# TensorE instructions in source order inside the long loops of a two-block transformer kernel

## The chip, the cores and the metric

One core of one Trainium2 chip runs the whole program. The metric is device time in microseconds (us), lower is better. TensorE (PE) does every matrix product and every transpose. VectorE (DVE) and ScalarE (ACT) do reductions, exponentials and copies out of PSUM, GpSimd (POOL) a few element-wise steps, and SyncE (SP) issues the transfers.

## The reference

Two transformer blocks on 256 latent tokens (and, in the first layer, 256 context tokens) of width 1024, all in fp32. What matters here, cut down:

```python
def first_block(...):                       # layer 0 and layer 1
    hl, hc = modulate(x_lat, ...), modulate(x_ctx, ...)          # RMS norm with adaptive scale and shift
    mix = even_mixer(...) or odd_mixer(...)                      # layer 0 or layer 1
    x = x + gate * (mix @ w_out[l])
    x = x + gate * conv_ffn(modulate(x), ffn_up, conv, ffn_down) # 1024 -> 2 x 2816 -> 1024
# even_mixer: four recurrent (mLSTM) heads, and eight heads of window attention over 512 tokens
# odd_mixer:  eight heads of global attention, and eight heads of neighbourhood attention with a bias
def window_attention(q, k, v, k_ctx, v_ctx, sink):
    s = [q @ k_ctx, mask(q @ k_band)]
    p = softmax([sink, s])                  # one row per query
    return p @ v
# second_block: mixer A (three dilated groups, merged by their log-sum-exp), layer norm, gate;
#               mixer B (window of 128 with sinks), layer norm, gate
```

## The kernel before, in words

**Products.** Every weight product is made of three matmuls in a reduced fp32 format: a weight is split into a high part (`whi`, cast by ACT at L396) and a low part (`wlo`, subtracted by DVE at L400, by POOL at L398), and hi times hi, hi times lo and lo times hi are summed in PSUM. `gemm_t` (L443, matmuls at L439 to L441 in `mm_t`) holds the weights still and streams the tokens, 512 or 256 columns at a time; `gemm_n` (L477, matmuls at L484 to L486) holds the tokens still. Weights come from memory through SP, 1 MB at a time, into two buffers, and are split in good time. The matmuls of the adaptive norm's parameters (L533, transposes L540) are strewn between.

**Attention.** `_attn_pair` (L841) makes one unit of attention: 128 queries, two heads, 128 to 512 keys. It has three pieces. `probs` issues the scores on PE (L800, L801, a mask at L860), the row maximum on DVE (L867, L870), the exponential on ACT (L882), sums, sinks and the reciprocal on DVE (L872 to L888), and divides the two heads' rows `P` by their sums, on DVE (L900) and on POOL (L901). `turn` transposes `P` on PE (L916, L927) into a tile `t` of PSUM and copies it out as `PT` (L920, L929 on DVE, L931 on ACT). `pv` multiplies `PT` by the values on PE (L937). Mixer A has its own scores (L1633). Tiles of PSUM are few: two for `t`, two for scores `s`, three for products `g`, one for `o`.

**The order of the work.** A hand-made pipe (`_Pipe`, L233) sets the order in which the source issues the pieces. Products call `tick` with their columns, and whenever `pace` columns are through (7000 in window attention, 12000, 9000 and 4000 in layer 1, 10000 in mixer A, 5000 in mixer B), `slot` (L258) issues the next piece of every unit under way, the oldest first, and then the scores of a new one:

```python
    def slot(self):
        for u in list(self.live):
            u.pop(0)()
            if not u:
                self.live.remove(u)
        if self.pending:
            early, u = self.pending.pop(0)
            ...
            u.pop(0)()
            self.live.append(u)
```

So in source order `pv` of one unit, the transposes of the next and the scores of the one after stand together, and between a unit's scores and its transposes there are the products of one or two ticks and the `pv` of the unit before it. In mixer B (`K.lag = 1`) a unit's transposes come one slot later. On top of this a scheduler goes over the whole program: it keeps what depends on what, and orders each engine's list of instructions by its own estimate of when they can start. In the kernel before it does this for all engines everywhere.

Of the kernel before, what the change touches and what calls it, by code (L numbers as in the profile page):

```python
# [10 lines left out]
F32 = mybir.dt.float32  # L11
# [294 lines left out]
class _K:  # L306
    def __init__(self, ctx, tc, aps, out, stop=None, dbg=None):
# [25 lines left out]
        self.sa = rows("sa", 2)  # L333
        self.tm = rows("tm", 6)
        self.n = 0

    def nm(self, s):
        self.n += 1
# [479 lines left out]
def _pow(K, out, ms, n):  # L818
    K.nc.gpsimd.tensor_tensor(out, ms, K.mhalf[:, 0:n], op=ALU.pow)
# [134 lines left out]
def _layer0(K):  # L954
# [3 lines left out]
    with tc.tile_pool(name="h0", bufs=1, reuse_waits="tile") as hp, ExitStack() as es:  # L958
# [32 lines left out]
        with tc.tile_pool(name="att0", bufs=4, reuse_waits="tile") as ap, tc.tile_pool(name="swa", bufs=1, reuse_waits="tile") as sp:  # L991
# [28 lines left out]
                    for t in range(4):  # L1020
                        swa(q, pr, t, o)

            K.pipe.pace = 7000
            _q_gqa(K, sp, H, rows[:, R_SWA:R_SWA + 64], axc, axs, (0, 2), units)
            for T, s in ((kT, 128.0 ** -0.5), (qT, 1.0)):
                for c in range(2):
                    K.gemm_t(K.w(), H, 512, lambda m, g: nc.scalar.activation(T[:, 2 * c + m], g, AF.Copy, scale=s))
            K.pipe.drain()
        with tc.tile_pool(name="mls", bufs=1, reuse_waits="tile") as mp:
            mp = _Rows(mp)  # L1030
            vN = mp.tile([128, 4, 4, 129], F32, name="vN")
# [28 lines left out]
                                                    (slice(4, 8), mixb[x].bitcast(F32))])  # L1060
                return
            st = K.stats(segs)
            _wout(K, 0, mixa, segs, 0, ((256, 512), (0, 256)), st, K.norm(st[0], 0, 1, segs[1], 256))
        K.flush_ada()
        if K.stop == "xm0":
            K.dump("xm0", K.xt)
# [16 lines left out]
def _wout(K, l, mix, segs, k0=0, parts=None, st=None, hooks=()):  # L1083
    nc = K.nc
    t0 = segs[0][0]

    def evac(m, g, lo=0, hi=512):
        for a, b, t in segs:
            if a - t0 < lo or b - t0 > hi:
                continue  # L1090
            x = K.xt[:, m, a:b]
            nc.vector.scalar_tensor_tensor(x, g[:, a - t0:b - t0], K.mod[l][:, 2, t, m:m + 1], x, op0=ALU.mult,
                                           op1=ALU.add)
            if st:
                K.stat_add(st[t], x)

    for c in range(2):
        K.gemm_t(K.w(), mix, segs[-1][1] - t0, lambda m, g, *r: evac(4 * c + m, g, *r), k0, parts if c else None,
                 hooks if c else ())


def _ffn(K, l, segs, st, nxt=None):
# [3 lines left out]
    with tc.tile_pool(name=f"f{l}", bufs=1, reuse_waits="tile") as pool, tc.tile_pool(name=f"fw{l}", bufs=3, reuse_waits="tile") as wx:  # L1106
# [65 lines left out]
                K.gemm_t(K.w(), parts[i], n, lambda m, g, *r: evac(4 * c + m, g, *r), 0, cuts,  # L1172
                         K.norm(st[0], l + 1, 0, segs[1], 256, 3) if st else ())

        K.wide = True
        for i in range(len(FPARTS)):
            up(i)
            if i:
                down(i - 1)
        K.lookahead = 0  # L1180
        K.wide = False
        nst = nxt(segs) if nxt else None
        down(len(FPARTS) - 1, nst)
        K.lookahead = 1
        K.wx = None
        K.flush_ada()
    K.dump(f"x{l}", K.xt)
# [89 lines left out]
def _layer1(K, st):  # L1277
# [5 lines left out]
    with tc.tile_pool(name="l1", bufs=1, reuse_waits="tile") as pool, \  # L1283
# [45 lines left out]
                for t in range(2):  # L1329
                    gqa(q, pr, t, o)  # L1330

        K.pipe.pace = 12000
        _q_gqa(K, pool, H, rows[:, R_GQA:R_GQA + 64], axc, axs, (2,), units)
        kg = pool.tile([128, 64], F32, name="nkg")
        nc.vector.tensor_mul(kg, rows[:, R_NA:R_NA + 64], rows[:, R_NA + 64:R_NA + 128])
        kT = [pool.tile([128, 4, 512], F32R, name=f"nkT{i}") for i in range(2)]
        qT = [pool.tile([128, 8, 256], F32R, name=f"nqT{i}") for i in range(2)]
        def na(pr, t):
            o = _Out(K, 128, 1, 128)
            sl = slice(128 - 128 * t, 256 - 128 * t)  # L1340
            _attn_pair(K, 512, [[x[:, 2 * pr + e, 128 * t:128 * t + 128] for x in qT] for e in range(2)],
                       [[kT[e][:, pr]] * 2 for e in range(2)],
                       lambda e, b: K.xt[:, 2 * b + pr // 2, 128 * (pr % 2) + 64 * e:128 * (pr % 2) + 64 * e + 64],
                       lambda: o()[:, 0], lambda: K.hilo(mix[0][:, 4 + pr, sl], mix[1][:, 4 + pr, sl], o()[:, 0]),
                       bias=lambda e: (256, nb[t][:, 2 * pr + e].rearrange("p k c -> p (k c)")), ident=J)

        for kind, c in ((0, 0), (2, 0), (1, 0), (0, 1), (2, 1), (1, 1)):
            W = K.w()
            for t in ((0, 1) if kind < 2 else (1,)):
                ps = K.pg(128, 2, 256)  # L1350
                for b in range(2):
                    K.gemm_n(W, H, 2 * t + b, ps[:, b])
                if kind == 1:
                    for b in range(2):
                        nc.scalar.copy(K.xt[:, 2 * (2 * t + b) + c, 0:256], ps[:, b])
                    continue
                p8 = ps.rearrange("p b (h d) -> p (b h) d", d=64)
                p4 = ps.rearrange("p b (h d) -> p b h d", d=64)
                ms = _rms8(K, p8, 8, "eighth" if kind == 2 else None)
                rr = K.small([128, 8], "rr")  # L1360
                _pow(K, rr, ms, 8)
                if kind == 0:
                    x = K.e(2, 256)
                    x8 = x.rearrange("p b (h d) -> p (b h) d", d=64)
                    nc.vector.tensor_mul(x8, p8, rr.unsqueeze(2).to_broadcast([128, 8, 64]))
                    nc.vector.tensor_mul(x8, x8, kg.unsqueeze(1).to_broadcast([128, 8, 64]))
                    K.pipe.defer(14000, lambda d=[y[:, 2 * c:2 * c + 2, 256 * t:256 * t + 256] for y in kT], x=x:
                                 _tpose_stack(K, d, x.rearrange("p b (h d) -> p b h d", d=64)))
                    continue
                r4 = rr.rearrange("p (b h) -> p b h", b=2)  # L1370

                def wr(o, hs):
                    for z in range(2):
                        nc.vector.tensor_tensor(o[:, :, :, z], p4[:, :, hs],
                                                r4[:, :, hs].unsqueeze(3).to_broadcast([128, 2, 2, 64]),
                                                op=ALU.mult)

                _stack_k(K, [y[:, 4 * c:4 * c + 4] for y in qT], wr, J)
            if kind == 1:
                for t in range(2):  # L1380
                    for pr in (2 * c, 2 * c + 1):
                        na(pr, t)
                K.pipe.pace = 9000
        K.pipe.settle(8, 8)
        K.pipe.pace = 4000
        _wout(K, 1, mix, lat)
        K.pipe.drain()
        if K.stop == "mix1":
            K.dump("mix1", mix[0].bitcast(F32)), K.dump("mix1l", mix[1].bitcast(F32))
            return  # L1390
# [177 lines left out]
def _block2a(K):  # L1568
# [3 lines left out]
    with tc.tile_pool(name="a2", bufs=1, reuse_waits="tile") as pool, tc.tile_pool(name="aw", bufs=2, reuse_waits="tile") as wx, ExitStack() as es:  # L1572
# [77 lines left out]
        def attn(hg, *a):  # L1650
            for pr in range(2):
                o = _Out(K, 128, 2, 128)
                for t in range(2):
                    unit(hg, pr, t, o, *a)

        K.pipe.pace = 10000
        for hg in range(4):
            attn(hg, *gemms(hg))
        _wout2(K, mx, xp, 0)
        K.pipe.drain()  # L1660
        es.close()
        K.wx = None
        pool2 = _Rows(es.enter_context(tc.tile_pool(name="a2b", bufs=1, reuse_waits="tile")))
# [8 lines left out]
def _block2b(K):  # L1672
# [3 lines left out]
    with tc.tile_pool(name="b2", bufs=1, reuse_waits="tile") as pool, tc.tile_pool(name="b2q", bufs=2, reuse_waits="tile") as qp, \  # L1676
# [63 lines left out]
                       nsink=nsink[:, h2], sink=rows[:, R_BSINK + 2 * kt:R_BSINK + 2 * kt + 2],  # L1740
                       masks=((0, m0),) if t == 0 else ((0, m1),), idm=idb)

        K.pipe.pace = 5000
        K.lag = 1
        for hg in range(4):
            qT = gemms(hg)
            for pr in range(2):
                o = _Out(K, 128, 2, 128)
                for t in range(2):
                    unit(hg, pr, t, o, qT)  # L1750
        _wout2(K, mx, xl, 0)
        K.pipe.drain()
        rb = _wout_ln(K, mx, xl, pool, 1)

        def fin(m, a, b):
# [73 lines left out]
```

## Time and profile before

| | us |
|---|---|
| median of three runs (1650.22 to 1658.45) | 1651.43 |
| the profiled execution | 1659.3 |
| its span | 1657.5 |
| PE busy | 1587.5 (96%) |
| PE loading weights | 1380.9 (83%) |
| DVE busy | 1126.1 (68%) |
| ACT busy | 776.5 (47%) |
| POOL busy | 262.8 (16%) |

Where the stages lie in the span, in us: window attention of layer 0 from 75 to 190, recurrent heads from 217 to 305, FFN from 343 to 740, norm of layer 1 to 760, attention of layer 1 to 925, its FFN to 1132, mixer A from 1180 to 1460, its layer norm and gate to 1535, mixer B to 1610, and the tail. The profile lists, for each engine, when it was busy and what ended each idle time; the table of windows gives busy time in chosen stretches, and a timeline gives single instructions with the idle time before them in brackets. A matmul's row ends later than the next one starts, since matmuls are pipelined: their pace is read from the starts.

### The profile page before, as it was taken

The page shows a single profiled execution, that of the slowest core. Times are in us where ns is not written, and L with a number is a line of the kernel's source. Part 1 is how long each engine was busy: PE and PEld are TensorE (multiplying, and loading weights), DVE is VectorE, ACT ScalarE, POOL GpSimd, SP SyncE. Part 2 cuts the span into 40 slices and gives each one's busy share as a digit, 9 for nine tenths or more (in the row PEclk, how much of TensorE's full clock was granted, in tenths as well). Part 3 has the DMA queues.
Part 4 walks back from the last instruction along what each step waited for, and adds up shares of the span by engine and source line. Part 5 has one row for each costly group of instructions (what it writes and reads, how often), then busy time and mean ns, then how long its engine had stood idle before and what let it go on. Part 6 is the DMA issues. An engine that isn't in the chain of part 4 may idle for free.

```text
span 1657.5 us, 28332 instructions
## 1 busy us (share of the span) xinstructions
PE 1587.5 (96%) x11406; PEld 1380.9 (83%) x11406; DVE 1126.1 (68%) x2169; ACT 776.5 (47%) x1431; POOL 262.8 (16%) x239
## 2 busy tenths in 40 slices
PE   5899999999999999999999899999999999989998
PEld 2777776787777788888888789999999999989887
DVE  4776355576646575577777798777676666677897
ACT  3454344454323333244555555554454554445554
POOL 2321000030000000005231344441010101120111
PEclk9999998999999999998999999999999999989999
DMA  8233321335544432323343355554525352416333
GB/s 333 86 126 103 108 74 59 136 140 175 178 153 176 180 127 102 102 91 94 106 124 128 129 202 187 195 191 157 178 102 179 103 178 102 159 56 214 102 103 102
DMA packets 43475, 229.57 MB, mean 139 GB/s; under 512 B 12552, under 2 KB 15752, under 8 KB 16464
## 3 DMA queue, kind: packets, MB, share of 16 engines
q1 hardware_dynamic: 43344, 227.76, 39.7%
q8 instruction: 90, 1.47, 0.3%
q14 instruction: 41, 0.34, 0.1%
HBM read 226.70 MB, written 1.05 MB: 137 GB/s over the span
## 4 chain that ended last, share of the span: by engine, by line
PE 81%; DVE 9%; DMA 3%; POOL 3%; ACT 3%; issue 2%; SPq 0%; POOLq 0%; DVEq 0%; ACTq 0%
PE g L439 11%; PE g L440 11%; PE g L441 11%; PE g L484 6%; PE g L486 6%; PE g L485 6%; PE s L439 4%; PE s L441 4%; PE s L440 4%; PE o L937 3%; DMA raw<-in_w_dram 3%; PE g L533 3%; DVE wlo L400 2%; PE t L927 2%; PE s L800 1%
## 5 line engine op out<-in xcount | busy, mean ns | idle before, releaser
L396 ACT CAST whi<-raw 128x1024 fp32r<-128x1024 f32 x322 | 332.3, 1048 | 284.2 <-DMA raw<-in_w_dram 179.9
L400 DVE TENSOR_TENSOR wlo<-raw,whi 128x1024 fp32r<-128x1024 f32 x289 | 357.4, 1245 | 141.4 <-ACT whi L396 135.6
L439 PE MATMUL g<-H,whi 128*128 128x256 f32 (+1 forms) x944 | 303.2, 324 | 5.2 <-ACT H L1477 1.8
L440 PE MATMUL g<-H,whi 128*128 128x256 f32 (+1 forms) x944 | 301.8, 320 | 5.5 <-DVE H L630 5.1
L484 PE MATMUL g<-whi,H 128*128 128x256 f32 x1040 | 300.1, 289 | 3.5 <-ACT H L635 2.0
L441 PE MATMUL g<-H,wlo 128*128 128x256 f32 (+1 forms) x944 | 299.3, 318 | 1.7 <-POOL wlo L398 1.7
L486 PE MATMUL g<-whi,H 128*128 128x256 f32 x1040 | 295.7, 285 | 2.4 <-DVE H L639 1.8
L485 PE MATMUL g<-wlo,H 128*128 128x256 f32 x1040 | 294.0, 283 | 0.5 <-DVE wlo L400 0.5
L484 PEld LDWEIGHTS g<-whi,H 128*128 128x128 f32 x1040 | 199.2, 192 | 11.1 <-issue 3.6
L486 PEld LDWEIGHTS g<-whi,H 128*128 128x128 f32 x1040 | 198.6, 191 | 4.8 <-DVE H L639 2.4
L485 PEld LDWEIGHTS g<-wlo,H 128*128 128x128 f32 x1040 | 199.3, 192 | 1.1 <-DVE wlo L400 0.8
L439 PEld LDWEIGHTS g<-H,whi 128*128 128x128 f32 x944 | 177.3, 189 | 26.0 <-issue 4.8
L440 PEld LDWEIGHTS g<-H,whi 128*128 128x128 f32 x944 | 178.3, 189 | 21.7 <-DVE H L630 9.1
L441 PEld LDWEIGHTS g<-H,wlo 128*128 128x128 f32 x944 | 178.0, 189 | 14.8 <-POOL wlo L398 2.1
L901 POOL TENSOR_SCALAR P<-P,rc 128x512 f32<-128x512 f32 (+2 forms) x64 | 55.2, 863 | 500.5 <-DVE rc L1639 263.6
L398 POOL TENSOR_TENSOR wlo<-raw,whi 128x1024 fp32r<-128x1024 f32 x33 | 81.2, 2459 | 100.4 <-ACT whi L396 97.5
L439 PE MATMUL s<-H,whi 128*128 128x256 f32 (+1 forms) x264 | 89.2, 338 | 0.0
L440 PE MATMUL s<-H,whi 128*128 128x256 f32 (+1 forms) x264 | 88.0, 333 | 0.0
L441 PE MATMUL s<-H,wlo 128*128 128x256 f32 (+1 forms) x264 | 87.9, 333 | 0.0
L439 PE MATMUL g<-G,whi 128*128 128x256 f32 (+1 forms) x240 | 78.9, 329 | 3.0 <-DVE e L1124 2.5
L440 PE MATMUL g<-G,whi 128*128 128x256 f32 (+1 forms) x240 | 77.8, 324 | 0.0
L441 PE MATMUL g<-G,wlo 128*128 128x256 f32 (+1 forms) x240 | 77.7, 324 | 0.0
(394 smaller groups left out, 2963.4 us busy)
## 6 DMA issues: line engine op xcount, KB each, us to landing
raw<-in_w_dram SPq DMA_DIRECT2D x209, 1024.0 KB, 4.9
xt<-in_xt_dram SPq DMA_DIRECT2D x1, 2048.0 KB
nab<-in_rpb_dram SPq DMA_DIRECT2D x16, 128.0 KB, 4.0
out_dram<-xt SPq DMA_DIRECT2D x4, 256.0 KB, 2.2
agw<-in_agw_dram SPq DMA_DIRECT2D x1, 512.0 KB, 20.3
mka<-in_tab_dram SPq DMA_DIRECT2D x1, 512.0 KB, 3.5
plr<-in_p_dram SPq DMA_DIRECT2D x2, 256.0 KB, 6.7
e<-in_tab_dram SPq DMA_DIRECT2D x5, 64.0 KB, 4.7
```

Of the source, the lines that this page charges most:

```text
L396: nc.scalar.copy(hi, raw)
L398: nc.gpsimd.tensor_tensor(lo, raw, hi.bitcast(F32), op=ALU.subtract)
L400: nc.vector.tensor_sub(lo, raw, hi.bitcast(F32))
L439: nc.tensor.matmul(out, hi[:, k, s], X[0][:, x], start=f, stop=False)
L440: nc.tensor.matmul(out, hi[:, k, s], X[1][:, x], start=False, stop=False)
L441: nc.tensor.matmul(out, lo[:, k, s], X[0][:, x], start=False, stop=l)
L484: nc.tensor.matmul(out, X[0][:, a + k, s], hi[:, k], start=f, stop=False)
L485: nc.tensor.matmul(out, X[0][:, a + k, s], lo[:, k], start=False, stop=False)
L486: nc.tensor.matmul(out, X[1][:, a + k, s], hi[:, k], start=False, stop=l)
L533: nc.tensor.matmul(acc[g:g + 32], self.sc[:, k, :], raw[:, k], start=(k < 4), stop=(k >= 4))
L901: nc.gpsimd.tensor_scalar(P[1], P[1], rc[:, 1:2], 0.0, op0=ALU.mult, op1=ALU.add)
L937: nc.tensor.matmul(o[64 * e:64 * e + 64], vv(e, b), u["T"][e][:, b], start=(b == 0), stop=(b == kb - 1))
```

## The change

A method `as_written` opens a region in which the scheduler leaves PE's instructions in the order in which the source issues them; the other engines, and the order between engines, stay with it. It is put around the loops of window attention in layer 0 (with the `drain` that empties the pipe), the output product of layer 0, the FFN of both layers, the whole attention of layer 1 with its output product, and the loops of mixers A and B. The norms, the recurrent heads and the layer-norm tails of mixers A and B stay outside. Nothing is added or removed: every engine has the same instructions as before. Names of lines are three to some nine higher in the changed kernel, since lines were added.

```diff
+    def as_written(self):
+        return self.tc.manual_schedule(engines={mybir.EngineType.PE})
...
+            with K.as_written():
+                K.pipe.pace = 7000
+                _q_gqa(K, sp, H, rows[:, R_SWA:R_SWA + 64], axc, axs, (0, 2), units)
...
+                K.pipe.drain()
...
+            with K.as_written():
+                _wout(K, 0, mixa, segs, 0, ((256, 512), (0, 256)), st, K.norm(st[0], 0, 1, segs[1], 256))
...
+        with K.as_written():
+            K.wide = True
+            for i in range(len(FPARTS)):
+                up(i)
+                if i:
+                    down(i - 1)
...
+        with K.as_written():
+            K.pipe.pace = 12000
+            _q_gqa(K, pool, H, rows[:, R_GQA:R_GQA + 64], axc, axs, (2,), units)
...
+            K.pipe.settle(8, 8)
+            K.pipe.pace = 4000
+            _wout(K, 1, mix, lat)
+            K.pipe.drain()
...
+        with K.as_written():
+            K.pipe.pace = 10000
+            for hg in range(4):
+                attn(hg, *gemms(hg))
+            _wout2(K, mx, xp, 0)
+            K.pipe.drain()
...
+        with K.as_written():
+            K.pipe.pace = 5000
+            K.lag = 1
...
+            _wout2(K, mx, xl, 0)
+            K.pipe.drain()
```

**Window attention, PE.** A unit of 512 keys has its scores in tiles `s_321` and `s_322`, its rows in `P_323` and `P_324`, its transposes in `t_327` and `t_329`; `s_333` holds the scores of the next unit, of 256 keys; `g_310` and `g_311` are products. Before:

```order
L801 MATMUL s_322_1681<-kT2_101_534,qT2_122_687 128x512
...
L439 MATMUL g_311_1639<-H0_99,whi_303_1617 128x512
...
L937 MATMUL o_291_1577<-PT_316_1670,v_100_533 64x128
L439 MATMUL g_310_1638<-H0_99,whi_305_1621 128x512
...
L800 MATMUL s_333_1740<-kT2_101_534,qT2_121_686 128x256
...
L440 MATMUL g_310_1638<-H1_100,whi_305_1621 128x512
L927 MATMUL t_327_1724<-ident_83,P_323_1692 128x128 x4
L927 MATMUL t_329_1731<-ident_83,P_324_1693 128x128 x4
L441 MATMUL g_310_1638<-H0_99,wlo_306_1622 128x512
```

Now:

```order
L804 MATMUL s_322_1683<-kT2_101_534,qT2_122_689 128x512
...
L442 MATMUL g_311_1641<-H0_99,whi_303_1619 128x512
...
L940 MATMUL o_291_1579<-PT_316_1672,v_100_533 64x128
L930 MATMUL t_327_1726<-ident_83,P_323_1694 128x128 x4
L930 MATMUL t_329_1733<-ident_83,P_324_1695 128x128 x4
L803 MATMUL s_333_1742<-kT2_101_534,qT2_121_688 128x256
...
L442 MATMUL g_310_1640<-H0_99,whi_305_1623 128x512
```

The transposes have moved ahead of the next unit's scores and of the products `g_310` (eleven of its matmuls stood before them). Between `s_322` and `t_327` there remain the 12 matmuls of `g_311` and the 8 of `pv`.

**The same unit, DVE, in the change.** `wlo_357` and `wlo_359` are low parts of a later weight, `nb` the row maxima.

```order
L873 TENSOR_REDUCE nb_318_1679<-s_321_1682 128x1
L873 TENSOR_REDUCE nb_318_1679<-s_322_1683 128x1
L403 TENSOR_TENSOR wlo_357_1865<-raw_355_1862,whi_356_1864 128x1024
L875 TENSOR_TENSOR nb_318_1679<-nb_318_1679,qnr_120_687 128x2
L403 TENSOR_TENSOR wlo_359_1869<-raw_355_1862,whi_358_1868 128x1024
L877 TENSOR_TENSOR nb_318_1679<-nb_318_1679,nsink_676 128x2
L888 TENSOR_TENSOR es_325_1698<-nb_318_1679,rows_101 128x2
L890 TENSOR_TENSOR ls_319_1680<-ls_319_1680,es_325_1698 128x2
L891 RECIPROCAL rc_320_1681<-ls_319_1680 128x2
L903 TENSOR_SCALAR P_323_1694<-P_323_1694,rc_320_1681 128x512
```

The two subtractions of a weight stand inside the unit's chain, as they did before; what moved is the work of the next unit, whose reduction stood between these rows and now follows them.

**Layer 1, neighbourhood attention, PE.** Here `J` is the matrix that transposes, `s_1502` and `s_1503` are the scores of the next to last unit, `t_1515` and `t_1517` its transposes, `g_1511`, `g_1512` and `g_1525` tiles of the output product (256 columns). Before:

```order
L801 MATMUL s_1503_8437<-nkT1_6973,nqT1_6975 128x512
L439 MATMUL g_1512_8477<-mix10_6770,whi_1468_8290 128x256
...
L927 MATMUL t_1496_8420<-J_6604,P_1491_8387 128x128 x4
L927 MATMUL t_1498_8427<-J_6604,P_1492_8388 128x128 x4
L439 MATMUL g_1525_8536<-mix10_6770,whi_1470_8294 128x256
...
L801 MATMUL s_1522_8520<-nkT1_6973,nqT1_6975 128x512
...
L440 MATMUL g_1525_8536<-mix11_6771,whi_1470_8294 128x256
L927 MATMUL t_1515_8503<-J_6604,P_1504_8446 128x128 x4
L927 MATMUL t_1517_8510<-J_6604,P_1505_8447 128x128 x4
```

Now:

```order
L930 MATMUL t_1496_8431<-J_6613,P_1491_8398 128x128 x4
L930 MATMUL t_1498_8438<-J_6613,P_1492_8399 128x128 x4
L803 MATMUL s_1502_8447<-nkT0_6983,nqT0_6985 128x512
...
L804 MATMUL s_1503_8448<-nkT1_6984,nqT1_6986 128x512
L442 MATMUL g_1511_8474<-mix10_6779,whi_1468_8301 128x256
...
L940 MATMUL o_1513_8502<-PT_1497_8437,xt_87 64x128
L930 MATMUL t_1515_8514<-J_6613,P_1504_8457 128x128 x4
L930 MATMUL t_1517_8521<-J_6613,P_1505_8458 128x128 x4
L803 MATMUL s_1521_8530<-nkT0_6983,nqT0_6985 128x512
```

Each unit's transposes now stand ahead of the next unit's scores, where before they stood behind them. The products between a unit's scores and its transposes are 24 matmuls for this unit, and 12 for the three others of the last four.

**Mixer B, PE.** `s_2714` holds the scores of a unit of 128 keys, `t_2728` its transposes, `t_2719` and `s_2723` belong to the units before and after it, `g_2735` is a product of the next group of heads. Before:

```order
L860 MATMUL s_2714_16116<-mb0b_15623,idb2_15629 128x128
L486 MATMUL g_2735_16202<-whi_2682_15968,H1_100 128x256
...
L860 MATMUL s_2723_16148<-mb1b_15627,idb2_15629 128x256
L484 MATMUL g_2735_16202<-whi_2682_15968,H0_99 128x256
...
L937 MATMUL o_2717_16135<-PT_2709_16108,vb_15693 64x128 x2
L916 MATMUL t_2719_16139<-ident_83,P_2705_16075 128x128 x4
...
L860 MATMUL s_2747_16250<-mb1b_15627,idb2_15629 128x256
L916 MATMUL t_2728_16176<-ident_83,P_2715_16125 128x128 x2
```

Now:

```order
L863 MATMUL s_2714_16136<-mb0b_15641,idb2_15647 128x128
L940 MATMUL o_2717_16155<-PT_2709_16128,vb_15711 64x128 x2
L919 MATMUL t_2719_16159<-ident_83,P_2705_16095 128x128 x4
L803 MATMUL s_2723_16168<-kTb0_15722,qTb_2679_15984 128x256
...
L863 MATMUL s_2723_16168<-mb1b_15645,idb2_15647 128x256
L940 MATMUL o_2717_16155<-PT_2718_16158,vb_15711 64x128 x4
L919 MATMUL t_2728_16196<-ident_83,P_2715_16145 128x128 x2
```

The matmuls of `g_2735` and the scores of two further units that stood before `t_2728` have moved behind it. Six matmuls of `pv`, four transposes and the scores of one unit are all that remains between this unit's scores and its transposes.

## Rows read from the trace of the kernel before

**Rows 1.** Windows: stretch, us, busy (count) of PE, PEld, DVE, ACT, POOL, PEclk, DMA, GB/s.

```profile
75.00:190.00 115.00, 114.36 (x827) 88.38 (x826) 76.20 (x197) 56.42 (x132) 21.62 (x27) 1.00 0.32 108
740.00:760.00 20.00, 17.89 (x105) 15.49 (x104) 15.23 (x47) 10.56 (x21) 11.98 (x16) 0.74 0.57 167
760.00:925.00 165.00, 157.69 (x1363) 140.56 (x1363) 125.34 (x238) 84.80 (x169) 43.83 (x37) 0.99 0.33 109
1180.00:1460.00 280.00, 279.71 (x2365) 264.02 (x2365) 183.13 (x290) 141.65 (x224) 24.70 (x24) 1.00 0.40 137
1535.00:1610.00 75.00, 74.12 (x628) 66.74 (x628) 65.46 (x176) 41.37 (x119) 10.76 (x16) 1.00 0.31 105
```

**Rows 2.** PE's timeline from 764: start, us, instruction, count, [idle before <-releaser].

```profile
765.45 0.28 PE L485 MATMUL g<-wlo,H 128*128 128x256 f32 x1
765.56 0.28 PE L486 MATMUL g<-whi,H 128*128 128x256 f32 x1
769.56 1.09 PE L1228 MATMUL t<-ident,e 128*128 128x128 f32 x4 [3.72 <-DVE e L1222]
770.30 0.56 PE L484 MATMUL g<-whi,H 128*128 128x256 f32 x1
```

**Rows 3.** Timeline of window attention, PE: two matmuls of a product, 512 columns.

```profile
151.31 0.40 PE L439 MATMUL g<-H,whi 128*128 128x512 f32 x1
151.54 0.39 PE L440 MATMUL g<-H,whi 128*128 128x512 f32 x1
```

**Rows 4.** Timeline of window attention: last scores, one pv, normalised rows of four units.

```profile
148.22 0.23 PE L860 MATMUL s<-sw1b,idb 128*128 128x128 bf16 x1
...
153.22 0.89 POOL L901 TENSOR_SCALAR P<-P,rc 128x512 f32<-128x512 f32 x1 [4.86 <-DVE rc L888]
...
156.28 0.23 PE L860 MATMUL s<-sw2b,idb 128*128 128x128 bf16 x1
...
159.26 1.09 PE L937 MATMUL o<-PT,v 128*64 128x128 f32 x16
...
161.44 0.28 PE L801 MATMUL s<-kT,qT 128*128 128x256 f32 x1
...
162.89 0.98 POOL L901 TENSOR_SCALAR P<-P,rc 128x512 f32<-128x512 f32 x1 [8.78 <-DVE nb L874]
...
165.22 0.54 POOL L901 TENSOR_SCALAR P<-P,rc 128x256 f32<-128x256 f32 x1 [1.35 <-ACT PT L931]
...
166.89 0.28 PE L801 MATMUL s<-kT,qT 128*128 128x256 f32 x1
...
171.87 0.34 DVE L900 TENSOR_SCALAR P<-P,rc 128x256 f32<-128x256 f32 x1
```

**Rows 5.** Timeline of neighbourhood attention: last scores and normalised rows of two units.

```profile
893.83 0.39 PE L801 MATMUL s<-nkT,nqT 128*128 128x512 f32 x1
...
897.24 0.40 PE L801 MATMUL s<-nkT,nqT 128*128 128x512 f32 x1
...
897.67 1.01 POOL L901 TENSOR_SCALAR P<-P,rc 128x512 f32<-128x512 f32 x1 [12.19 <-PE s L801]
...
903.47 0.96 POOL L901 TENSOR_SCALAR P<-P,rc 128x512 f32<-128x512 f32 x1 [4.79 <-DVE mix L639]
```

**Rows 6.** Timeline of mixer A: last scores and normalised rows of one unit.

```profile
1217.50 0.71 PE L1633 MATMUL s<-kTa,qTa 64*128 64x128 f32 x4
...
1222.52 0.98 POOL L901 TENSOR_SCALAR P<-P,rc 128x512 f32<-128x512 f32 x1 [7.57 <-DVE rc L1639]
```

**Rows 7.** Timeline of mixer B: last score and normalised rows of a unit, 128 keys.

```profile
1546.95 0.23 PE L860 MATMUL s<-mb0b,idb 128*128 128x128 bf16 x1
...
1553.62 0.37 POOL L901 TENSOR_SCALAR P<-P,rc 128x128 f32<-128x128 f32 x1 [3.54 <-DVE es L885]
```

**Rows 8.** Timeline of the first FFN's start, DVE: first and last low part of H.

```profile
357.25 0.43 DVE L630 TENSOR_TENSOR H<-e,H 128x256 fp32r<-128x256 f32 x1 [0.46 <-POOL e L629]
...
363.85 0.43 DVE L630 TENSOR_TENSOR H<-e,H 128x256 fp32r<-128x256 f32 x1 [0.46 <-POOL e L629]
```

More of the change, by code (lines that the diff above doesn't have):

```diff
@@ L1021, in units @@
                         swa(q, pr, t, o)
[L1023 to L1028, printed above, removed]
+            with K.as_written():
+                K.pipe.pace = 7000
+                _q_gqa(K, sp, H, rows[:, R_SWA:R_SWA + 64], axc, axs, (0, 2), units)
+                for T, s in ((kT, 128.0 ** -0.5), (qT, 1.0)):
+                    for c in range(2):
+                        K.gemm_t(K.w(), H, 512, lambda m, g: nc.scalar.activation(T[:, 2 * c + m], g, AF.Copy, scale=s))
+                K.pipe.drain()
         with tc.tile_pool(name="mls", bufs=1, reuse_waits="tile") as mp:
@@ L1062, in _layer0 @@
             st = K.stats(segs)
-            _wout(K, 0, mixa, segs, 0, ((256, 512), (0, 256)), st, K.norm(st[0], 0, 1, segs[1], 256))
+            with K.as_written():
+                _wout(K, 0, mixa, segs, 0, ((256, 512), (0, 256)), st, K.norm(st[0], 0, 1, segs[1], 256))
         K.flush_ada()
@@ L1173, in down @@
                          K.norm(st[0], l + 1, 0, segs[1], 256, 3) if st else ())
[L1175 to L1184, printed above, removed]
+        with K.as_written():
[4 more added lines that the diff above has]
+                    down(i - 1)
+            K.lookahead = 0
+            K.wide = False
+            nst = nxt(segs) if nxt else None
+            down(len(FPARTS) - 1, nst)
+            K.lookahead = 1
         K.wx = None
@@ L1330, in units @@
                     gqa(q, pr, t, o)
[L1332 to L1352, printed above, removed]
-                if kind == 1:
[L1354 to L1383, printed above, removed]
@@ L1654, in attn @@
                     unit(hg, pr, t, o, *a)
[L1656 to L1660, printed above, removed]
+        with K.as_written():
[4 more added lines that the diff above has]
+            K.pipe.drain()
         es.close()
@@ L1741, in unit @@
                        masks=((0, m0),) if t == 0 else ((0, m1),), idm=idb)
[L1743 to L1752, printed above, removed]
+        with K.as_written():
+            K.pipe.pace = 5000
+            K.lag = 1
+            for hg in range(4):
+                qT = gemms(hg)
+                for pr in range(2):
+                    o = _Out(K, 128, 2, 128)
+                    for t in range(2):
+                        unit(hg, pr, t, o, qT)
+            _wout2(K, mx, xl, 0)
+            K.pipe.drain()
         rb = _wout_ln(K, mx, xl, pool, 1)
```

50 lines of the change are left out of this document (46 added, 4 removed).

## Prediction

> **What bounds the kernel now.** I read the table of windows first, because the change touches loops and leaves the norms alone, and each loop has to be judged by itself. In it the reader is to compare PE's busy time with the length of the stretch: 114.36 of 115 us in window attention, 157.69 of 165 in layer 1's attention, 279.71 of 280 in mixer A, 74.12 of 75 in mixer B [rows 1]. TensorE is the bound in all four, and what it idles there is 0.6 + 7.3 + 0.3 + 0.9 = 9.1 us. That is all a better order could take out.
>
> Next I read PE's timeline where one wait is long. A transpose waits 3.72 us for VectorE, and behind it a product's matmul, of the same line and tile as those before it, comes at 770.30, only after it [rows 2]. So matmuls start in the order of the list: an instruction that stands in it before its operand is there costs PE the whole rest of the wait, whatever is ready behind. The scheduler had filled such times with products. The question is therefore, for every unit of attention: is the work that the new list leaves between its scores and its transposes as long as its softmax takes?
>
> The two lengths come from the timelines. Work: matmuls of a product with 512 columns start 0.23 us apart [rows 3], with 256 columns 0.11 us [rows 2], and a `pv` of eight matmuls takes 1.09 us [rows 4]. Softmax: from the end of a unit's last score to the end of its later normalisation (POOL's, once DVE's), when both rows of `P` are there.
>
> **The terms.** The number of matmuls in between is counted in the new list.
>
> *Window attention, layer 0.* 16 units, as four pairs of heads with the same four units [rows 4]:
> - 512 keys: scores end at 156.51, `P` at 163.87, so 7.36 us. The new list leaves 12 matmuls and a `pv`: 12 x 0.23 + 1.09 = 3.85. Short by 3.5. DVE's list still has two weight subtractions inside this chain, so I do not expect it to shrink by itself.
> - 256 keys: 161.72 to 165.76, 4.04 against the same 3.85. Short by 0.2.
> - 256 keys: 167.17 to 172.21, 5.04 against 12 matmuls and half a `pv`, 3.3. Short by 1.7.
> - 512 keys: 148.45 to 154.11, 5.66 against 12 matmuls, half a `pv` and ten small matmuls of the adaptive norm, which I count like a product's: 5.6. Short by 0.1.
>
> Sum 5.5, times four: **22 us**. If both 512-key units took the shorter 5.66 and both others 4.04, it would be 2.8 x 4 = 11; if they took the longer 7.36 and 5.04 (short by 3.5, 1.2, 1.7 and 1.8), 33.
>
> *Layer 1's attention.* Its last four units stand beside the output product with 256 columns only: 12 matmuls alone, 12 and a `pv`, 24 and a `pv`, 12 and a `pv`, or 1.3, 2.4, 3.7 and 2.4 us. Two of these softmaxes [rows 5]: 894.22 to 898.68, 4.46 us, and 897.64 to 904.43, 6.79 us. At the shorter all four are short by 3.2 + 2.1 + 0.8 + 2.1 = 8.2, at the longer by 5.5 + 4.4 + 3.1 + 4.4 = 17.4. I take 11.5, nearer the shorter, since the longer one has a weight's subtraction to wait for. Of the other twelve units two have 24 matmuls and a `pv` and ten about twice as many (6.4 us): at 4.46 us that is 2 x 0.8 = 1.6, at 6.79 it is 2 x 3.1 + 10 x 0.4 = 10. I take the middle, 5.5. Together **17 us**, between 10 and 27.
>
> *Mixer A.* 16 units with 24 matmuls and a `pv`, 3.7 us. One of the longer softmaxes goes from 1218.21 to 1223.50, 5.29 us [rows 6]: short by 1.6. The shortest at hand, 4.04 us [rows 4], is short by 0.3. These are the ends, 5 and 26 us; I take the middle, 0.95 each, since units of both kinds alternate here: **15 us**.
>
> *Mixer B.* 16 units. One of 128 keys takes from 1547.18 to 1553.99, 6.81 us [rows 7]. In the first group of heads the new list leaves it no product, only some 18 short matmuls (at 0.11 us, 2.0): short by 4.8. The products that stood there before belonged to the next group. Later groups keep 24 to 36 of their own, 4 us more, and come out even. With the extra slot two units' softmaxes run at once, so a wait serves both: two waits for the four units of the first group, **9 us**; one wait is 4.8, four are 19.
>
> *Starts of the FFNs.* The low parts of H come one `k` at a time, the first ending at 357.68, the eighth at 364.28, so 6.6 us [rows 8]. Before, several tiles of products were mixed `k` by `k` with them. In the new list one tile's 24 matmuls of 0.11 us, 2.6, stand first: 4.0 short. The second FFN has half as many tokens and only two tiles to mix; I take 1.5 for it, between 0 and the same 4.0. Together **5.5 us**, 3 to 8. The rest of the FFN loops has no unit to wait for: nothing.
>
> *Gained.* Of the 9.1 us idle in the loops, 3.72 [rows 2] hang on a chain through VectorE that is not shortened. The other **5.4 us** go; the ends are 0 and 9.1.
>
> DMA, splits and copies are the same instructions in nearly the same order; a TensorE that waits only gives them time.
>
> Sum: 22 + 17 + 15 + 9 + 5.5 - 5.4 = **63 us**; the lower ends give 11 + 10 + 5 + 5 + 3 - 9 = 25, the upper ones 33 + 27 + 26 + 19 + 8 = 113. The durations are those of the profiled execution of 1659.3 us, 0.5% above the median of 1651.43. The difference is carried over to the median: **1714 us**, 1676 to 1764.
>
> **Rivals.**
>
> *TensorE has room that its busy time hides, so the waits cost nothing.* Weight loads fill 88.38 of 115, 140.56 of 165, 264.02 of 280 and 66.74 of 75 us [rows 1], which leaves 26.6 + 24.4 + 16 + 8.3 = 75 us, more than the 63. If PE could use that to catch up after a wait, the time stays at some 1651. For it: a matmul's row is longer (0.40) than the distance to the next one. Against it: that distance is 0.23 in an undisturbed product [rows 3], so the stream itself sets the pace and nothing is caught up later. I give it 0.07. [...]
>
> *The softmaxes get shorter, and the kernel faster.* In the new list both heads' scores stand together, where before other matmuls had come between them in places, and VectorE has less of the next unit to mix in. If every `P` is there within the 3.7 us of cover, all waits vanish and the 9.1 us are gained: 1642. It decides at that point, and the shortest softmax, 4.04 [rows 4], is only a little above it. Against it: 512 keys took 5.66 at best, and the weight subtractions stay inside the chains. 0.06.
>
> *The clock falls as well.* [...] Against it: layer 1's attention shows 0.99 with 7.3 us idle [rows 1]. 0.20. [...]
>
> *The change does not do what it says.* The three places shown from the new list exclude it.
>
> **Numbers.** Forecast 0.67, clock 0.20, hidden room 0.07, shorter softmaxes 0.06. A run of this kernel can be told from no change at about 0.5%, 8 us. Faster is the rival of 1642: 0.06; same is that of 1651: 0.07; slower the other two: 0.87. The range holds the forecast's own (1676 to 1764), goes a little below it, to 1668, for units whose waits cover each other, and to 1768 for the clock; what is left out is the two rivals on the fast side, 0.13, and the longest of the clock's times.
>
> **What would show it.** In the profile after: a transpose of `P` (L930, or L919) that waits for DVE or POOL in most units, by 3 to 4 us in window attention's first 512-key unit of each pair, by 2 to 4 in the last four of layer 1, by about 1 in mixer A and by about 5 in mixer B's first group; PE's busy time in these loops unchanged, and its idle time up by about 63; the first FFN's start about 4 us later at the same work. The granted clock tells the third rival. Wrong it would be if PE's list shows waits on `P` below 1 us in window attention, or if the same waits stand there and the stage ends no later.

## The result and the profile after

The changed kernel takes 1724.91 us (median of four runs, 1719.95 to 1727.95), the kernel before, beside it, 1652.03. The ratio is 1.0431, 95% interval 1.0392 to 1.0470: 71 us slower. Forecast were 1714 us in a range of 1668 to 1768, and 0.87 for slower. Ratios here and below are of undisturbed executions; one of the eight of the FFN run, at 3060 us, is not among them.

The profiled execution of the change is the shortest of its four (1719.95, span 1718.2), that of before a long one (1659.3, span 1657.5), so the two traces are 60.7 us apart, 10 less than the medians. The head of the page after, with its engines and the first line of its chain:

```profile
PE 1588.0 (92%) x11406; PEld 1386.9 (81%) x11406; DVE 1132.5 (66%) x2169; ACT 777.6 (45%) x1431; POOL 259.3 (15%) x239
...
PE 72%; DVE 10%; DMA 3%; ACT 3%; POOL 3%; issue 2%; POOLq 0%; ACTq 0%; DVEq 0%; SPq 0%
```

TensorE's busy time was 1587.5 before and is 1588.0 now, for the same work. In sum, the added time is time in which it waits; by stages it is not quite so.

Where that is, the windows tell. Both tables are cut at the same places of the program, so their rows correspond to within a few matmuls: window attention, recurrent heads, layer 1's attention, mixer A, mixer B (columns as in [rows 1]). Before:

```profile
75.00:196.00 121.00, 120.36 (x876) 93.16 (x875) 76.90 (x198) 57.41 (x134) 21.62 (x27) 1.00 0.32 108
196.00:341.00 145.00, 142.12 (x828) 111.22 (x825) 76.88 (x197) 65.95 (x179) 4.04 (x4) 0.94 0.28 99
...
774.20:919.50 145.30, 141.76 (x1244) 125.03 (x1242) 109.08 (x214) 74.67 (x151) 35.62 (x30) 1.00 0.36 121
...
1148.70:1458.00 309.30, 309.03 (x2622) 293.45 (x2620) 202.21 (x314) 156.25 (x243) 24.70 (x24) 1.00 0.41 141
...
1535.40:1612.90 77.50, 76.62 (x650) 69.24 (x649) 67.66 (x184) 42.82 (x123) 10.76 (x16) 1.00 0.32 110
```

After:

```profile
73.00:216.20 143.20, 123.75 (x874) 97.33 (x873) 82.08 (x199) 59.47 (x135) 22.11 (x27) 0.94 0.27 93
216.20:353.90 137.70, 134.00 (x826) 105.95 (x825) 74.95 (x195) 64.14 (x177) 4.04 (x4) 1.00 0.29 100
...
788.10:951.70 163.60, 142.28 (x1244) 124.98 (x1243) 111.26 (x215) 75.41 (x153) 38.26 (x31) 0.99 0.32 107
...
1183.70:1501.30 317.60, 308.38 (x2622) 292.54 (x2619) 203.18 (x314) 156.42 (x243) 20.60 (x24) 1.00 0.40 137
...
1582.50:1674.00 91.50, 81.18 (x648) 73.98 (x648) 69.22 (x177) 41.65 (x116) 7.98 (x15) 0.92 0.27 93
```

The four loops grew by 22.2, 18.3, 8.3 and 14.0 us, 62.8 together. Idle time of TensorE in them (length less busy time) rose from 0.6, 3.5, 0.3 and 0.9 to 19.5, 21.3, 9.2 and 10.3 us. In window attention and mixer B its busy time rose too, by 3.4 and 4.6 us for the same matmuls, and there the granted clock is 0.94 and 0.92 where it was 1.00. The recurrent heads, which the change does not touch, are 7.3 us shorter: their clock was 0.94 in the trace of before and is 1.00 now, so this goes with the clock of the execution and not with the order. Their busy time is 8.1 us less, about what the two loops have more, so that the sums of busy time agree partly by chance.

What TensorE waits for, over the whole execution (engine, line and tile, releaser: us in total, times, longest):

```profile
PE t L930 <- DVE P L903: 25.6, 16, 5.6
...
PE t L919 <- DVE P L903: 7.5, 5, 3.3
PE s L803 <- DVE qTb L798: 5.8, 2, 3.8
...
PE t L1412 <- ACT PT L934: 4.0, 5, 1.3
...
PE t L1234 <- DVE e L1228: 2.6, 1, 2.6
PE t L1541 <- DVE PT L932: 2.5, 8, 0.3
PE t L1541 <- DVE rc L891: 2.4, 1, 2.4
PE t L543 <- DVE qT L799: 2.4, 1, 2.4
PE t L1541 <- DVE ls L890: 2.3, 1, 2.3
```

The transposes of `P` (L930, L919) lead with 33 us, 35 with those that wait for POOL's row; the trace of before has 3.4 of both kinds in the four loops. But there are others that the forecast did not have: the first scores of a group that wait for its q (L803), transposes of q and k that wait for VectorE or, where the releaser is a copy `PT`, for a free one of the two PSUM tiles `t` (L1412, L1541). Of the first scores' waits, one of 3.8 us lies ahead of the cut for mixer B, in the stretch of mixer A's layer norm and gate, which grew from 77.4 to 81.2 us; mixer B's row leaves it out.

The kind of unit that the prediction began with, the second one of 512 keys of a pair of heads, in the timeline of the change: last score, `pv`, normalisation on DVE and on POOL, transposes, then products.

```profile
172.65 0.23 PE L863 MATMUL s<-sw2b,idb 128*128 128x128 bf16 x1
...
175.63 1.09 PE L940 MATMUL o<-PT,v 128*64 128x128 f32 x16
...
178.36 0.49 DVE L903 TENSOR_SCALAR P<-P,rc 128x512 f32<-128x512 f32 x1
178.42 0.99 POOL L904 TENSOR_SCALAR P<-P,rc 128x512 f32<-128x512 f32 x1 [7.92 <-DVE rc L891]
178.99 1.36 PE L930 MATMUL t<-ident,P 128*128 128x128 f32 x8 [2.27 <-DVE P L903]
...
181.00 0.63 PE L442 MATMUL g<-H,whi 128*128 128x512 f32 x1
181.43 0.63 PE L443 MATMUL g<-H,whi 128*128 128x512 f32 x1
```

Twelve products and the `pv` are through at 176.72, and TensorE stands still for 2.27 us until DVE's row of `P` is there. And the products after it start 0.43 us apart, not 0.23 [rows 3]: the granted clock is 0.50 from 180 to 183, where it was 1.00 from 172 to 176.7, so the wait costs more than it lasts.

The longest wait for `P` belongs to a unit of which the prediction expected next to none, the first one of 512 keys in the first pair of heads:

```profile
115.25 1.94 PE L930 MATMUL t<-ident,P 128*128 128x128 f32 x8 [5.63 <-DVE P L903]
```

In the first pair no product stands between this unit's scores, through at 108.0, and its transposes, only 16 short matmuls of the adaptive norm and half a `pv`, 1.6 us together.

### The profile page after: what moved, and what is told of

It is laid out like the page before. It is cut to its first block, busy times and chain, and to the rows that moved or that the text cites. A ratio compares the mean times of both kernels' runs of the same rounds, so it can differ in the third digit from the quotient of the medians.

```text
span 1718.2 us, 28344 instructions
## 1 busy us (share of the span) xinstructions
PE 1588.0 (92%) x11406; PEld 1386.9 (81%) x11406; DVE 1132.5 (66%) x2169; ACT 777.6 (45%) x1431; POOL 259.3 (15%) x239
## 4 chain that ended last, share of the span: by engine, by line
PE 72%; DVE 10%; DMA 3%; ACT 3%; POOL 3%; issue 2%; POOLq 0%; ACTq 0%; DVEq 0%; SPq 0%
PE g L442 10%; PE g L443 10%; PE g L444 10%; PE g L487 6%; PE g L489 5%; PE g L488 5%; PE s L442 4%; PE s L443 4%; PE s L444 4%; DMA raw<-in_w_dram 3%; DVE wlo L403 3%; PE o L940 2%; PE t L930 2%; PE g L536 1%; PE s L803 1%
## 5 line engine op out<-in xcount | busy, mean ns | idle before, releaser
L442 PE MATMUL g<-H,whi 128*128 128x256 f32 (+1 forms) x944 | 307.1, 327 | 6.8 <-ACT H L1484 1.8
L443 PE MATMUL g<-H,whi 128*128 128x256 f32 (+1 forms) x944 | 304.4, 323 | 6.3 <-DVE H L633 5.7
L487 PEld LDWEIGHTS g<-whi,H 128*128 128x128 f32 x1040 | 202.2, 194 | 10.6 <-issue 3.6
L489 PEld LDWEIGHTS g<-whi,H 128*128 128x128 f32 x1040 | 201.4, 194 | 8.3 <-DVE H L633 5.2
L442 PEld LDWEIGHTS g<-H,whi 128*128 128x128 f32 x944 | 179.9, 191 | 27.0 <-issue 3.6
L443 PEld LDWEIGHTS g<-H,whi 128*128 128x128 f32 x944 | 180.2, 191 | 23.4 <-DVE H L633 10.7
```

The lines of the kernel that those rows point to most:

```text
L442: nc.tensor.matmul(out, hi[:, k, s], X[0][:, x], start=f, stop=False)
L443: nc.tensor.matmul(out, hi[:, k, s], X[1][:, x], start=False, stop=False)
L487: nc.tensor.matmul(out, X[0][:, a + k, s], hi[:, k], start=f, stop=False)
L489: nc.tensor.matmul(out, X[1][:, a + k, s], hi[:, k], start=False, stop=l)
```

## The experiments

Ratios are to the kernel before, run beside each on the same chip; us are worked out on 1652.

### One loop at a time, and the FFNs

The region is kept in one place, and is empty in the others. In the run for window attention, for example, at the FFNs:

```diff
-        with K.as_written():
+        with nullcontext():
             K.wide = True
```

and so at the other places; `only_ffn` keeps it for the FFNs and layer 0's output product.

> Source order on TensorE in layer 0's window attention alone, the rest free as before. Theory (a transpose of P that stands in the list before its softmax is done costs the rest of the wait, where no work is left between): as in the profile of the whole change, where this stretch ends 22 us later; so 1652 + 22 = 1674, with 18 to 20 us more idle time of TensorE in this stretch and the rest unmoved. Rival (the loops slow each other: later stages start from a worse state, or the granted clock falls): less than half of it alone, under 1663. Rival (the time goes with the number of matmuls that are ordered): this stretch has 830 of some 9300 ordered, so 1652 + 73 x 0.09 = 1659.

> Source order in layer 1's attention alone. Theory: 18 us as in the whole change's profile, so 1670. Rival (loops slow each other, or the clock): under 1661. Rival (by number of matmuls, 1360 of 9300): 1663.

> Source order in mixer A's loop alone. Theory: 8 us as in the whole change's profile (I had predicted 15), so 1660. Rival (by number of matmuls, 2620 of 9300): 1672. Rival (loops slow each other, or the clock): 1652 to 1656.

> Source order in mixer B's loop alone. Theory: 14 us as in the whole change's profile (I had predicted 9), of which 9 idle time and 5 a lower clock, so 1666, or 1661 if the clock holds here. Rival (by number of matmuls, 650 of 9300): 1657.

> Source order in the FFN loops of both layers and layer 0's output product alone. Theory (only uncovered waits cost, and here these are the two starts, where H comes piece by piece): 0 to 4 us by the whole change's profile (2.3 at the first start, 0.9 at the second; I had predicted 5.5), so 1653 to 1657, though some 3100 of the 9300 ordered matmuls are here. Rival (by number of matmuls): 1652 + 73 x 0.34 = 1677.

| region kept | ratio, 95% interval | us | predicted term |
|---|---|---|---|
| window attention | 1.0122 (1.0105 to 1.0139) | 20.2 | 22 |
| layer 1's attention | 1.0154 (1.0122 to 1.0185) | 25.4 | 17 |
| mixer A | 1.0048 (1.0033 to 1.0062) | 7.9 | 15 |
| mixer B | 1.0106 (1.0091 to 1.0121) | 17.5 | 9 |
| FFNs | 1.0034 (1.0013 to 1.0055) | 5.6 | 5.5 |

Together 76.6 us, against 71 (65 to 78) for the whole change: the parts add up, each loop is slower by itself, and the rival in which they slow each other falls. So does the one by which the cost goes with the number of matmuls: the FFNs have a third of them and a thirteenth of the cost. Three sizes were outside what I expected for these runs. The FFNs' is so by less than its interval. Mixer B's stretch in the profile of the change had been cut behind the wait of 3.8 us for q, which explains most of the difference (17.5 against 14.0). Layer 1's stretch, from its first to its last normalisation on POOL, takes 145.0 us in the run with layer 1 alone and 140.0 in the change, with the granted clock at 0.96 and 0.99; so part of its 25.4 is the clock of these executions, one of which took 1688 us where the other three took 1677 to 1680.

### Transposes that do not need P

In both branches of `turn`, in the whole change:

```diff
-                    nc.tensor.transpose(tp[:, e, b], P[e][:, 128 * b:128 * b + 128], ident)
+                    nc.tensor.transpose(tp[:, e, b], K.ident, ident)
```

> Source order in all loops, and every transpose of an attention unit reads the identity in place of its softmax rows P, so it needn't wait for them; the softmaxes are still computed, but left out of the result. Nothing is added or taken from TensorE's work or order. Theory (the transposes' waits for P are the cost): of the 73 us some 5 to 15 are left (starts of the FFNs, tiles of PSUM, scores that wait for a free tile), so 1657 to 1670. Rival (the order itself costs: products torn from their weights, PSUM tiles, the clock): nearly all stays, 1710 to 1727.

Ratio 1.0160 (1.0125 to 1.0195), 26 us slower than before, where the change is 71 slower. So 45 us (36 to 53 by the two intervals) hang on the waits for `P`: the larger part, as the theory has it, but the rest is more than the 5 to 15 us that I expected. The edit also frees the buffers of `P` earlier, since no transpose reads them; this run can't tell that from the waits themselves. By loops, in us from the first to the last normalisation on POOL, which all three kernels do:

| | before | change | transposes without P |
|---|---|---|---|
| window attention | 87.6 | 109.3 | 87.8 |
| layer 1's attention | 124.8 | 140.0 | 135.3 |
| mixer A | 246.5 | 255.5 | 250.4 |
| mixer B | 63.2 | 83.6 | 77.9 |

So the waits for `P` are all of the loss in window attention and about half in mixer A, but only a third or less of it in layer 1 and in mixer B. What is left to wait for in layer 1's attention of that run:

```profile
PE t L1412 <- ACT PT L934: 3.1, 2, 2.0
PE t L1541 <- DVE PT L932: 2.8, 4, 1.3
PE t L1412 <- DVE PT L932: 2.5, 2, 2.2
PE s L803 <- DVE qT L798: 2.0, 1, 2.0
```

Three of the four rows are transposes of q and k that wait until a copy has emptied a PSUM tile `t`.

### Layer 1: the two PSUM tiles

In layer 1's attention alone, the transposes of q and k (`_stack_k`, `_tpose_stack`) get tiles of the products:

```diff
-        tp = K.pt(128, 2, 2, 128)
+        tp = K.pd(128, 2, 2, 128)
...
+    def pd(self, *shape):
+        return self.psum("g", shape, 3) if self.turns_in_g else self.pt(*shape)
```

> Source order in layer 1's attention alone, and the transposes of its q and k (not those of P) go into the three PSUM tiles of the products instead of the two that they share with the transposes of P. In the profile of source order in layer 1 alone TensorE waits about 12 us for P and about 7 us for a free one of these two tiles, since in source order the transposes of q and k stand right behind those of P. Theory (the two tiles are a second cost beside the softmax): those 7 us go, less a wait or two for a tile of the products, so 4 to 7 us below 1678, ratio 1.010 to 1.013 to the kernel before. Rival (only the waits for P cost, and the others are waited out behind them anyway): 1.0154 as before, or more.

Ratio 1.0065 (1.0043 to 1.0088), where the same region without this edit has 1.0154: some 15 us of the 25 go (8 to 21 by the two intervals), more than I expected. The waits of the run without the edit, layer 1's stretch:

```profile
PE t L930 <- DVE P L903: 11.0, 8, 2.6
PE s L803 <- DVE qT L798: 2.0, 1, 2.0
PE t L1412 <- ACT PT L934: 2.0, 2, 1.2
PE t L1412 <- DVE PT L932: 1.3, 2, 0.9
PE t L1541 <- DVE PT L932: 1.3, 4, 0.3
...
PE t L1541 <- ACT PT L934: 1.0, 1, 1.0
```

and with it:

```profile
PE t L934 <- DVE P L907: 10.4, 7, 2.8
PE s L807 <- DVE qT L802: 2.0, 1, 2.0
PE g L448 <- POOL wlo L405: 1.7, 1, 1.7
PE t L547 <- ACT PT L938: 1.3, 2, 0.7
```

The wait for `P` is as long as before the edit, so the softmaxes are untouched; the transposes of q and k (5.6 us of rows with `PT`) wait no more. The two profiled spans are 11.5 us apart (1675.2 and 1663.7), and the stretch from the first to the last normalisation on POOL 9.8 (145.0 and 135.2). The rows explain half of that. The granted clock over layer 1 rose from 0.96 (of 165 us) to 0.98 (of 158 us), by estimate from these a fall of 3.4 us in what is lost to it; this half was not separated from the edit. The stretch is left at 135.2 us, and without the waits for `P` it was left at 135.3: neither edit alone brings back the 124.8 of before.

### Mixer B: the transposes of q earlier

In mixer B alone:

```diff
-            K.pipe.defer(14000, lambda: _tpose_stack(K, qT, q))
+            K.pipe.defer(6000, lambda: _tpose_stack(K, qT, q))
```

> Source order in mixer B's loop alone, and the transposes of a group's q come after 6000 columns of the next product, where they came behind all of it, right ahead of the first scores that read them. In the profile of source order in mixer B alone, softmax rows P are the smaller part of what TensorE waits for: the first scores of the first and third group wait for q (about 4 and 2.6 us), the transposes of q of the second and fourth for VectorE (2.5 each), transposes of P and pv about 4. Theory (any instruction that stands ahead of its operand costs the rest of the wait, units of attention or not): the first two waits go, 5 to 6 us of the 17.5, so 1665 to 1668. Rival (only the units' own waits cost): no change, 1672 (1671 to 1674).

Ratio 1.0044 (1.0028 to 1.0061), from 1.0106: 10 us of the 17.5 go (7 to 14 by the two intervals), more than the 5 to 6 that I expected. Mixer B's waits without this edit:

```profile
PE s L803 <- DVE qTb L798: 6.0, 2, 4.0
PE t L1541 <- DVE rc L891: 2.4, 1, 2.4
PE t L1541 <- DVE ls L890: 2.3, 1, 2.3
PE t L919 <- DVE P L903: 1.7, 1, 1.7
```

and with it:

```profile
PE t L1541 <- DVE ls L890: 4.6, 2, 2.3
PE o L940 <- DVE e L1558: 2.1, 1, 2.1
PE t L1541 <- DVE e L1513: 1.6, 2, 0.9
PE t L919 <- DVE es L888: 1.1, 1, 1.1
```

The first scores no longer wait for q. The two profiled spans are 6.8 us apart (1670.0 and 1663.2), and all waits of TensorE in the stretch add up to 14.3 and 9.4 us, so the rows account for half of the 10; the rest is not assigned. These are not waits of a unit of attention at all: in the source the transposes of a group's q stand at the end of its products, right ahead of the scores, and the 14000 columns after which they were to come are more than that product has (2 x 24 x 256 = 12288). The free order had put the products of the next group there.

### Transposes one slot later

In the whole change, and for control in the kernel before; mixer B goes from 1 to 2. A fourth buffer for `P` makes room:

```diff
-        self.lag = 0
+        self.lag = 1
...
-        return self.ap.tile([128, 512], F32, tag=tag, name=self.nm(tag))
+        return self.ap.tile([128, 512], F32, tag=tag, name=self.nm(tag), **({"bufs": 4} if tag == "P" else {}))
```

> Source order in all loops, and the transposes of every unit come one slot later (one more slot of products between scores and transposes; a fourth buffer for P where there were three). Theory: a slot is 2.7 us or more of products, most waits on P were 1 to 4 us, so two thirds of them go, in part into waits of the next scores for a free tile of scores: 1670 to 1695. Rival (the order itself costs): as the change, 1715 to 1730.

> The same later transposes in the kernel before, all free: the control for the run with source order. Theory: the scheduler had already filled these waits, so no change, 1648 to 1662. Rival (the later transposes are a gain or a loss of their own, whatever the order): below 1645 or above 1665.

In source order: 1.0299 (1.0267 to 1.0332), 49 us slower than before, 22 less than the change but short of what I expected. By the normalisations on POOL, window attention is back at 89 us (109 in the change, 88 before) and layer 1's attention at 132 (140 and 125), while mixer A takes 262, more than the change's 256 (247 before). There a new wait has come:

```profile
PE t L1412 <- DVE e L1619: 6.8, 3, 2.4
```

The transposes of mixer A's keys now stand ahead of VectorE's work on them. Source order gives each instruction one place, and a shift that covers one operand uncovers another. The new wait only takes the place of the old ones, though: TensorE idles for 7.6 us between these marks and for 7.3 in the change. What is longer is its busy time, at a lower granted clock, in the slowest of the four executions (below, the change):

```profile
1222.00:1484.40 262.40, 254.85 (x2082) 240.61 (x2080) 166.11 (x264) 126.34 (x200) 18.37 (x23) 0.95 0.38 129
```

```profile
1239.50:1495.10 255.60, 248.34 (x2115) 234.19 (x2114) 165.81 (x264) 126.05 (x200) 18.97 (x23) 1.00 0.38 133
```

In the free order the same edit makes the kernel faster: 0.9935 (0.9910 to 0.9960). I expected no change there, and was wrong; two runs were made to see why.

> The kernel before, all free, with a fourth buffer for P where there were three (layer 1 and mixer A), no later transposes. Control for the run that was faster, 1641: theory (the later transposes give the scheduler more to fill with; the buffer alone does nothing): 1650 to 1654. Rival (the buffer is the gain): 1641 to 1646.

> The kernel before, all free, fourth buffer, transposes one slot later in window attention, layer 1 and mixer A, but as before in mixer B. By the stages of the run that was faster (window attention 5 us shorter, layer 1's attention 5, mixer A 3, mixer B none): the same gain or more, 1638 to 1643, if it comes from these three. Rival (the gain is in mixer B or its state): 1648 to 1653.

The buffer alone does nothing: 0.9994 (0.9978 to 1.0011). The later transposes in window attention, layer 1 and mixer A, without mixer B, give 0.9918 (0.9892 to 0.9945), 13.5 us faster than before. With mixer B's it was 0.9935, and the intervals overlap: which of the two is faster is open. These are the fastest versions here, and they have no source order in them. The engines of the run with the buffer alone, and below them those of the run without mixer B:

```profile
PE 1585.5 (96%) x11406; PEld 1381.1 (84%) x11406; DVE 1127.6 (68%) x2169; ACT 776.4 (47%) x1431; POOL 260.8 (16%) x239
```

```profile
PE 1571.3 (96%) x11406; PEld 1374.2 (84%) x11406; DVE 1128.2 (69%) x2169; ACT 776.6 (47%) x1431; POOL 257.0 (16%) x239
```

TensorE is not idle for less time (68.6 us against 64.7); the same matmuls take 14 us less. By estimate up to 5 of these can be the clock, which averaged 0.984 with the buffer alone and 0.987 here (0.003 of some 1640 us). From the first score of window attention to its last `pv`, at a granted clock of 1.00 in both, TensorE changes 96 times from one kind of tile written (products, scores, transposes, `pv`) to another with the buffer alone, and 79 times here, and the time from the last start of one kind to the first of the next adds up to 18.8 us there and 13.0 here. That the scheduler needs fewer small fillers when the transposes are due later fits this; it was not tested by itself.

## Why the prediction was right, and where its steps were not

**The step that carried it** was that an instruction which stands in TensorE's list ahead of its operand costs the rest of the wait, and that the new list leaves too little work between scores and transposes. That is shown: 45 of 71 us go when the transposes do not need `P`, and window attention falls back to its old length by that edit, and by the later transposes too. The timeline has the wait at the kind of unit that was worked out. That the sum came within 8 us of the 71 is in part luck: only in window attention do the waits for `P` make the loss, and elsewhere terms that were too large and operands that were not looked at made up for each other.

**Window attention, 22 us: right in sum, by luck in its parts** (20.2; 22.2 in the profile). Of the four units of a pair, the second one of 512 keys was to be short by 3.5 us (the prediction's signs call it the first); it waits 2.28 and 2.27 in the second and third pair. The work in between was as counted (172.88 to 176.72, 3.84 us against 3.85). But I took the end of the softmax from POOL's row, and the first four transposes read DVE's, which is there 0.56 us earlier (178.85 and 179.41); and to POOL's row it was 6.5 us, not 7.4. The only other unit that waits in these pairs does so for 0.83 us, so that a pair costs 3.1 us and not 5.5, and the last one 0.8. What these lacked, others made up: 9.9 us of waits in the first pair, which I had counted like the rest and where less work lies in between (3.33, 0.91 and 5.63), 2.4 for a transpose of the adaptive norm, and the lower clock (0.94 over the stretch).

**Layer 1, 17 us: too small** (25.4). The waits for `P`, for which the 17 stood, are 11 us in its rows, and without them the stretch is only 4.7 us shorter; so that term was too large (and the middle of its 1.6 and 10 is 5.8, not 5.5). The step that failed counted only units of attention as waiting. The transposes of q and k, which source order puts right behind those of `P`, wait for one of two PSUM tiles; giving them others takes back some 15 us, of which the profile shows 9.8 in this stretch, and a part of that is the clock (0.96 without this edit, 0.98 with it).

**Mixer A, 15 us: too large** (7.9). I had taken the middle between a softmax that was short by 1.6 and one by 0.3. Its rows show 4.7 us of waits for `P` in 5 places, and 3.0 for PSUM tiles: most of the 16 units are covered. The lower end, 5, was the nearer.

**Mixer B, 9 us: too small, and for the wrong reason** (17.5). Units do wait for `P`, but for 2.5 us in all and not 9; that a wait for one unit is time for the next may be why. The larger part is the first scores' wait for q and the transposes of q, which I did not look at, 11 us in the rows of the run with mixer B alone; an edit that only moves the transposes of q takes back 10.

**Starts of the FFNs, 5.5 us: right within the noise** (5.6, 2 to 9). In the profile of the change the two starts are 2.3 and 0.9 us longer, where 4.0 and 1.5 were forecast.

**Gained, 5.4 us: not seen.** The long wait of 3.72 us [rows 2] stays, as 2.6 and 1.3 us in two pieces; the small waits for `P` that were to go grew instead.

**The rivals.** That TensorE has hidden room is refuted: 19 us of new waits in window attention are 22 us of time. That softmaxes shrink below their cover did not happen. The clock was rightly a rival but wrongly a separate case: it fell behind some waits and not behind others (0.76 over the 7 us from 179, behind a wait of 2.27 us, and 1.00 over the 4 us behind one of 2.28), and has its part in the forecast's own result with some 8 us of busy time (3.4 in window attention and 4.6 in mixer B). The top of the range, 1768, allows for a clock term that no run shows; these 8 us are what the profile of the change shows in its place.

## What to carry to other kernels

Before fixing one engine's order by hand, list every instruction on it whose operand comes from another engine (transposes of q and k and first readers as well as the softmax), and compare the work that the list leaves ahead of each with the time its producer takes; buffers that are reused belong to the list. Where that work is short, the engine waits (for `P` up to 5.63 us at a time here), and a free order that fills from the next group of work is worth keeping. When a scheduler is there, moving a consumer later in the source (here by one slot, with a buffer more) can pay, by 0.8% here, even though TensorE was hardly ever idle.

## What the runs showed of the hardware that I had not expected

After the wait of 2.27 us in window attention TensorE's granted clock was 0.50 from 180 to 183 and 1.00 again from 184: its products started 0.43 us apart instead of 0.23, and the granted clock from 179 to 186 averaged 0.76:

```profile
179.00:186.00 7.00, 7.00 (x41) 5.69 (x42) 2.55 (x8) 2.48 (x7) 0.96 (x2) 0.76 0.18 75
```

After a wait as long, before the same work and in the same execution 26 us earlier, it did not fall (the wait, and a row of the table of windows from its end on):

```profile
153.44 1.12 PE L930 MATMUL t<-ident,P 128*128 128x128 f32 x8 [2.28 <-DVE P L903]
```

```profile
153.44:157.50 4.06, 4.06 (x24) 3.42 (x24) 1.87 (x5) 1.83 (x6) 0.41 (x1) 1.00 0.29 117
```

In layer 1's attention, with more idle time in all (21.3 us), the clock averaged 0.99 in the change, and 0.96 where layer 1 alone was in source order. So in these runs an uncovered wait cost its length, and at times more in a slower clock (0.24 of the 7 us above, or an estimated 1.7 us), and neither the sum of the waits nor the length of one told which.
